# A mixture-of-experts layer on one core: the last expert's second product, combination and stores by halves of the columns

## Chip, cores, metric

One NeuronCore of a Trainium2 chip runs the whole layer in one launch. The metric is the device time of one execution in microseconds, as the median of several runs. The engines are TensorE (PE, its weight loads PEld), VectorE (DVE), ScalarE (ACT), GpSimd (POOL) and SyncE (SP), which issues the transfers that are spoken of here.

## What is computed

A layer over 512 latent tokens of 1024 channels with 256 context tokens: a DeltaNet mixer and latent attention, merged and added to the residual, and then sixteen experts of which each chooses 64 of the 512 tokens. The change touches the experts alone, and there the last of them:

```python
def expert_choice_moe(h, router_w, w_gate, w_up, w_down):
    cap = EC_CAPACITY * n_tok // N_EXPERTS                      # 64
    affinity = jax.nn.softmax((h @ router_w).astype(F32), axis=-1)
    gate, idx = lax.top_k(jnp.swapaxes(affinity, 1, 2), cap)
    xe = jax.vmap(lambda hb, ib: hb[ib])(h, idx)
    hid = jax.nn.silu(jnp.einsum('becd,edf->becf', xe, w_gate)) * jnp.einsum('becd,edf->becf', xe, w_up)
    ye = jnp.einsum('becf,efd->becd', hid, w_down) * gate[..., None].astype(h.dtype)
    return jax.vmap(lambda ib, yb: jnp.zeros((n_tok, d), yb.dtype).at[ib.reshape(-1)].add(yb.reshape(-1, d)))(idx, ye)

x = x_mid + mod_x[5] * expert_choice_moe(h2, ...)
```

w_gate and w_up are 1024 x 1408 per expert, w_down is 1408 x 1024, all in 32-bit floats.

## The kernel before

The experts run one after the other, from expert 0 to 15 (the loop at L1730). SP loads each expert's weights through a ring of nine buffers of 3072 columns (`piece`, L1709): four pieces of w_gate, four of w_up (each two blocks of 128 rows), then w_down in pieces of three blocks and a rest. A piece's transfer waits until TensorE is done with what lay in its buffer nine pieces before.

For an expert, TensorE multiplies its 64 tokens (XE, 128 rows by 64 columns of weights for the array) with w_gate into the PSUM tiles pg and with w_up into pu: the *first product*. The array is used as two halves of 64 columns each: the lower half of a row of weights goes to PSUM rows 0 to 63 (L1750), the upper to rows 64 to 127 (L1751), the two in turn, as pieces of 320 and 448 columns. ScalarE and VectorE make silu(pg) * pu of it in hd (L1769, L1771), TensorE turns it into hT by transposes (tile pt, L1774 to L1778, copied by L1775 to L1780).

The *second product* (tile pd, L1791) is hT times w_down: eleven blocks of 128 rows, and for each block columns 0 to 511 go to rows 0 to 63 of pd and columns 512 to 1023 to rows 64 to 127, again in turn:

```python
for dh in range(2):
    nc.tensor.matmul(pd[64 * dh:64 * dh + 64], l_, w[:, j, dh * 512:(dh + 1) * 512],
                     start=(i == 0), stop=(i == 10))
```

VectorE scales pd by gate and channel factor (L1795), ScalarE rounds the result to the type of the fast matmul (L1796), and VectorE takes the difference (L1797), so that the tile yo holds a high and a low part. The *combination* (tile pc, L1807) spreads the 64 rows over the 512 tokens: for each of four token tiles t and each half dh of the columns, one matmul of the high and one of the low part with the one-hot matrix oT; the rows of half dh lie on partitions 64 dh to 64 dh + 63. VectorE adds pc to the residual xm[t] (L1811). Experts are combined in pairs; 14 and 15 each by themselves. pc has two buffers of the tag "c"; expert 15's combination also borrows those of pg and pu. After expert 15 each half tile is stored as soon as it is added (L1813). A half tile is written (t, dh) below.

Apart from those lines of the program that are recorded through `TE`, `SE`, `VE` (a wrapper, `_Pinned`, that keeps an engine's instructions in program order among themselves and against what stands before them), the order on each engine is set by the tile scheduler, which lets matmuls of the next expert's first product stand between those of a combination.

Of the kernel before, what the change touches and what calls it, by code (L numbers as in the profile page):

```python
# [11 lines left out]
F32 = mybir.dt.float32  # L12
# [8 lines left out]
P = 128  # L21
# [11 lines left out]
NE = 16  # L33
# [141 lines left out]
def hybrid_block(ctx: ExitStack, tc: tile.TileContext, I, out, dbg=None):  # L175
# [1551 lines left out]
    GSTEP.update({(e, "w_gate", k0): 1 for e in (1, 2, 4, 5, 8, 9) for k0 in (0, 4)})  # L1727
    CH = ((0, 320), (320, 448))
    ys_ = []
    for e in range(NE):  # L1730
        pg = [pe([P, 448], "g", f"pg{e}{c}") for c in range(2)]
        pu = [pe([P, 448], "u", f"pu{e}{c}") for c in range(2)]
        for nm, dst in (("w_gate", pg), ("w_up", pu)):
            ko = (2, 4, 6, 0) if e == 0 and nm == "w_gate" else (0, 2, 4, 6)
            for k0 in ko:
                for _ in range(GSTEP.get((e, nm, k0), 0)):
                    next(ga, None)
                src = I[nm][0, e, k0 * P:(k0 + 2) * P, :].rearrange("(k p) f -> p k f", p=P)
                if e == 0 and nm == "w_gate" and k0 in (0, 6):
                    w = [halves[k0], halves[k0 + 1]]  # L1740
                else:
                    w = piece(FF, f"{nm}{e}_{k0}")
                    with tc.issue_after(issued["half" if PRM["p2"] else "woraw16"]):
                        nc.sync.dma_start(w, src)
                    w = [w[:, kk] for kk in range(2)]
                for kk in range(2):
                    k = k0 + kk
                    x_ = XE[:, e // GE % 2, k, (e % GE) * CAP:(e % GE + 1) * CAP]
                    for c, (o, n) in enumerate(CH):
                        nc.tensor.matmul(dst[c][0:64, :n], x_, w[kk][:, o:o + n], start=(k == ko[0]), stop=(k == ko[3] + 1))  # L1750
                        nc.tensor.matmul(dst[c][64:128, :320], x_, w[kk][:, FA + c * 320:FA + c * 320 + 320],  # L1751
                                         start=(k == ko[0]), stop=(k == ko[3] + 1))
        og = ex.tile([P, 4, 2, CAP], F32, tag="og", name=f"og{e}")
        for t in range(4):
            nc.vector.tensor_scalar(og[:, t], K("iota").unsqueeze(1).to_broadcast([P, 2, CAP]), slot[:, t, e:e + 1],
                                    aff[:, t, e:e + 1], op0=OP.is_equal, op1=OP.mult)
        p_ = pe([P, 4, P], "t", f"pog{e}", 1)
        for t in range(4):
            nc.tensor.transpose(p_[:, t], og[:, t].rearrange("p d s -> p (d s)"), ident)
        yo = ex.tile([P, 3, 512], F32R, tag="yo", name=f"yo{e}", bufs=2)  # L1760
        oT = yo[:, 2].rearrange("p (t s) -> p t s", t=4)
        nc.vector.tensor_scalar(oT, p_, 0.0, None, op0=OP.is_gt)
        gs = ex.tile([P, 1], F32, tag="gs", name=f"gs{e}", bufs=2)
        nc.vector.reduce_sum(gs, p_.rearrange("p t s -> p (t s)"), axis=AX.X)
        hh = ex.tile([P, 2, FA], F32, tag="hd", name=f"hd{e}", bufs=2)
        hd, hT = hh[:, 0], hh[:, 1].rearrange("p (b m) -> p b m", m=P)
        regs = ((0, slice(0, 128), 0, 320, 0), (1, slice(0, 128), 0, 320, 320), (1, slice(0, 64), 320, 448, 640))
        for c, pr, a, b, o in regs:
            nc.scalar.activation(hd[pr, o:o + b - a], pg[c][pr, a:b], AF.Silu)  # L1769
        for c, pr, a, b, o in regs:  # L1770
            nc.vector.tensor_mul(hd[pr, o:o + b - a], hd[pr, o:o + b - a], pu[c][pr, a:b])  # L1771
        p_ = pe([P, 4, P], "t", f"pt{e}0", 1)
        for b in range(4):
            nc.tensor.transpose(p_[:, b], hd[:, b * P:(b + 1) * P], ident)  # L1774
        nc.vector.tensor_copy(hT[:, 0:4], p_)  # L1775
        p_ = pe([P, 4, P], "t", f"pt{e}1", 1)
        nc.tensor.transpose(p_[:, 0], hd[:, 4 * P:5 * P], ident)
        nc.tensor.transpose(p_[:, 1, 0:64], hd[0:64, 5 * P:6 * P], ident[0:64, 0:64])  # L1778
        nc.vector.tensor_copy(hT[:, 4], p_[:, 0])
        nc.vector.tensor_copy(hT[:, 5, 0:64], p_[:, 1, 0:64])  # L1780
        pd = pe([P, 512], "d", f"pd{e}", 1)
        order = [(0, b) for b in range(6)] + [(1, b) for b in range(5)]
        for i0, n in ((0, 3), (3, 3), (6, 3), (9, 2)) if e < NE - 1 else ((0, 3), (3, 3), (6, 3), (9, 1), (10, 1)):
            w = piece(D, f"wd{e}_{i0}")
            nc.sync.dma_start(w[:, :n], I["w_down"][0, e, i0 * P:(i0 + n) * P, :].rearrange("(k p) d -> p k d", p=P))
            for j in range(n):
                i = i0 + j
                half, b = order[i]
                l_ = hT[:, b, half * 64:half * 64 + 64]
# [3 lines that stand above are left out]
        y = yo  # L1793
        yf = hd[:, 0:512]
        nc.vector.scalar_tensor_tensor(yf, pd, gs, m5, op0=OP.mult, op1=OP.mult)  # L1795
        nc.scalar.activation(y[:, 0], yf, AF.Copy)  # L1796
        nc.vector.tensor_sub(y[:, 1], yf, y[:, 0].bitcast(F32))  # L1797
        ys_.append((y, oT))
        if e % 2 or e == 14:
            for t in range(4):  # L1800
                tag = "cguc"[t] if e == 15 else "c"
                pcs = [pe([P, 512], tag, f"pc{e}{t}{dh}") for dh in range(2)]
                for i, (y_, o_) in enumerate(ys_):
                    for l in range(2):
                        for dh in range(2):
                            ps_ = slice(64 * dh, 64 * dh + 64)
                            nc.tensor.matmul(pcs[dh], o_[ps_, t, :], y_[ps_, l, :],  # L1807
                                             start=(i + l == 0), stop=(i + l == len(ys_)))
                for dh in range(2):
                    sl = slice(dh * 512, (dh + 1) * 512)  # L1810
                    nc.vector.tensor_add(xm[t][:, sl], xm[t][:, sl], pcs[dh])  # L1811
                    if e == NE - 1:
                        nc.sync.dma_start(out[0, t * P:(t + 1) * P, sl], xm[t][:, sl])  # L1813
            ys_ = []


# [22 lines left out]
```

## Time and profile before

| | |
|---|---|
| median of 3 runs | 1757.81 us (1753.52 to 1760.07) |
| the profiled execution | 1760.15 us |
| its span, first to last instruction | 1758.2 us |
| PE busy | 1590.3 us (90%) |
| DVE, ACT, POOL busy | 871.2, 593.5, 249.8 us |
| HBM read | 366.51 MB |

The page gives busy time by engine, the span in 40 slices, the chain of work that ended last, and the costliest groups of instructions. A timeline row has the start in us from the span's start, the time that it covers in us, engine, line, operation, output and inputs, rows and columns of the weights, rows and columns of the streamed operand, the count of records merged into it, and in brackets how long its engine stood idle before it and for what. A matmul in plain 32-bit floats leaves two records. The granted clock (PEclk) is a share of 2.4 GHz: 1.00 is 2.4 GHz, 0.50 is 1.2 GHz.

### The profile page before, as it was taken

To read this page: it belongs to the slowest core of one execution; us is meant where nothing else is said; L and a number is where in the kernel's file an instruction comes from. 1 tells how busy PE (TensorE), PEld (TensorE's weight loads), DVE (VectorE), ACT (ScalarE), POOL (GpSimd) and SP (SyncE) were. 2 spreads that over 40 slices of the span, in tenths; PEclk is the share of its full clock that TensorE was granted. 3 is DMA by queue.
4 is the path that set the end of the run, shared out by engine and by line. 5 is a ranking of instruction groups with operands and counts; after the bars stand their busy time and mean duration, and the time that the engine had idled before them with its cause. 6 is when DMAs were issued, how large, how long until landed. Compare 5 with 4: busy or idle time off the path is not lost.

```text
span 1758.2 us, 25301 instructions
## 1 busy us (share of the span) xinstructions
PE 1590.3 (90%) x9990; PEld 1096.7 (62%) x9990; DVE 871.2 (50%) x1926; ACT 593.5 (34%) x1362; POOL 249.8 (14%) x330
## 2 busy tenths in 40 slices
PE   5999998997999997989899996999999999989897
PEld 4687897785788786767687775544444454434343
DVE  3588758856978663757773446131212122212122
ACT  4676437425554344655674323100000010000000
POOL 2322022112121023222202522000000000000000
PEclk8999999998999998999899998999999999999999
DMA  9121302342222442030127945899999999999997
GB/s 324 49 61 37 110 24 61 96 145 84 61 67 79 136 138 66 26 109 21 46 72 234 287 171 208 328 413 412 413 412 413 413 413 413 413 413 413 414 413 288
DMA packets 168408, 382.30 MB, mean 217 GB/s; under 512 B 10373, under 2 KB 91491, under 8 KB 168291
## 3 DMA queue, kind: packets, MB, share of 16 engines
q1 hardware_dynamic: 163328, 372.98, 56.9%
q10 hardware_dynamic: 4963, 7.72, 1.4%
q8 instruction: 78, 1.28, 0.3%
q14 instruction: 39, 0.32, 0.1%
HBM read 366.51 MB, written 14.16 MB: 217 GB/s over the span
## 4 chain that ended last, share of the span: by engine, by line
PE 50%; DVE 9%; DMA 8%; ACT 4%; issue 3%; POOL 2%; SPq 0%; DVEq 0%; ACTq 0%; POOLq 0%
PE pd L1791 8%; PE pg L1750 6%; PE pu L1750 5%; DMA wd<-in_w_down_dram 4%; PE pg L1751 3%; PE pu L1751 3%; PE pc L1807 2%; DMA w_up<-in_w_up_dram 1%; PE pxe L1693 1%; PE pxe L1694 1%; PE px L140 1%; PE px L141 1%; PE px L142 1%; PE pPT L1337 1%; DMA raw_ukv<-in_w_ukv_dram 1%
## 5 line engine op out<-in xcount | busy, mean ns | idle before, releaser
L1750 PE MATMUL pg<-w_gate,XE 128*64 128x320 f32 x496 | 176.3, 505 | 1.1 <-DMA w_gate<-in_w_gate_dram 1.1
L1750 PE MATMUL pu<-w_up,XE 128*64 128x320 f32 x480 | 160.1, 487 | 5.2 <-DMA w_up<-in_w_up_dram 5.2
L1771 DVE TENSOR_TENSOR hd<-hd,pu 128x320 f32<-128x320 f32 (+1 forms) x48 | 18.6, 416 | 287.1 <-PE pu L1751 269.9
L1751 PE MATMUL pg<-w_gate,XE 128*64 128x320 f32 x496 | 154.0, 449 | 0.0
L1751 PE MATMUL pu<-w_up,XE 128*64 128x320 f32 x480 | 153.1, 444 | 0.0
L1791 PE MATMUL pd<-wd,hd 128*64 128x512 f32 x668 | 150.8, 597 | 1.6 <-DMA wd<-in_w_down_dram 1.6
L1796 ACT ACTIVATE yo<-hd 128x512 fp32r<-128x512 f32 x16 | 10.1, 629 | 344.2 <-DVE hd L1795 344.2
L1750 PEld LDWEIGHTS pu<-w_up,XE 128*64 128x64 f32 x480 | 64.6, 137 | 75.3 <-issue 37.3
L1791 PEld LDWEIGHTS pd<-wd,hd 128*64 128x64 f32 x668 | 44.8, 136 | 85.3 <-issue 76.0
L1750 PEld LDWEIGHTS pg<-w_gate,XE 128*64 128x64 f32 x496 | 65.8, 140 | 46.1 <-issue 23.2
L1769 ACT ACTIVATE hd<-pg 128x320 f32<-128x320 f32 (+1 forms) x48 | 16.5, 377 | 171.3 <-PE pg L1751 171.3
L1751 PEld LDWEIGHTS pg<-w_gate,XE 128*64 128x64 f32 x496 | 59.6, 137 | 23.2 <-issue 9.2
L1807 PE MATMUL pc<-yo 64*128 64x512 f32 x256 | 46.7, 450 | 26.1 <-ACT yo L1796 22.7
L1807 PEld LDWEIGHTS pc<-yo 64*128 64x128 f32 x256 | 23.1, 193 | 66.6 <-ACT yo L1796 35.9
L1811 DVE TENSOR_TENSOR xm<-xm,pc 128x512 f32<-128x512 f32 x72 | 45.9, 683 | 32.1 <-PE pc L1807 32.1
L1795 DVE SCALAR_TENSOR_TENSOR hd<-pd,gs,m 128x512 f32<-128x512 f32 x16 | 12.0, 751 | 96.3 <-PE pd L1791 96.3
L1697 ACT ACTIVATE XE<-pxe,mod,gs 128x256 f32<-128x256 f32 x32 | 16.3, 561 | 110.9 <-PE pxe L1694 98.2
L140 PE MATMUL pl_gt<-ht,wh_gt 128*128 128x512 f32 x128 | 52.6, 411 | 0.0
L142 PE MATMUL pl_gt<-ht,wl_gt 128*128 128x512 f32 x128 | 52.0, 406 | 0.0
L1751 PEld LDWEIGHTS pu<-w_up,XE 128*64 128x64 f32 x480 | 50.0, 135 | 3.1
L141 PE MATMUL pl_gt<-ht,wh_gt 128*128 128x512 f32 x128 | 51.4, 401 | 0.0
L1186 DVE TENSOR_TENSOR PT<-pPT,PT 128x512 fp32r<-128x512 f32 x48 | 33.0, 687 | 25.0 <-ACT PT L1185 24.8
(630 smaller groups left out, 4211.0 us busy)
## 6 DMA issues: line engine op xcount, KB each, us to landing
w_gate<-in_w_gate_dram SPq DMA_DIRECT2D x60, 1408.0 KB, 16.7
w_up<-in_w_up_dram SPq DMA_DIRECT2D x60, 1408.0 KB, 21.5
wd<-in_w_down_dram SPq DMA_DIRECT2D x45, 1536.0 KB
aw<-in_ada_w_dram SPq DMA_DIRECT2D x32, 512.0 KB, 4.7
wd<-in_w_down_dram SPq DMA_DIRECT2D x15, 1024.0 KB, 16.8
aq<-in_ada_w_dram SPq DMA_DIRECT2D x8, 1024.0 KB, 8.5
raw_gt<-in_w_in_dram SPq DMA_DIRECT2D x16, 512.0 KB, 3.8
ring_w<-in_w_up_dram SPq DMA_DIRECT2D x3, 1408.0 KB, 12.2
```

What stands on the lines that cost most here:

```text
L140: nc.tensor.matmul(out, wh, xh, start=first, stop=False)
L141: nc.tensor.matmul(out, wh, xl, start=False, stop=False)
L142: nc.tensor.matmul(out, wl, xh, start=False, stop=last)
L1186: nc.vector.tensor_sub(lo, src, hi.bitcast(F32))
L1337: nc.tensor.transpose(p_[:, t * P:(t + 1) * P], Pm[:, t, kt_ * P:(kt_ + 1) * P], ident)
L1693: nc.tensor.matmul(px[:, j], X2[:, t, 0, ks], oh, start=(t == 0), stop=False)
L1750: nc.tensor.matmul(dst[c][0:64, :n], x_, w[kk][:, o:o + n], start=(k == ko[0]), stop=(k == ko[3] + 1))
L1751: nc.tensor.matmul(dst[c][64:128, :320], x_, w[kk][:, FA + c * 320:FA + c * 320 + 320], start=(k == ko[0]), stop=(k == ko[3] + 1))
L1771: nc.vector.tensor_mul(hd[pr, o:o + b - a], hd[pr, o:o + b - a], pu[c][pr, a:b])
L1791: nc.tensor.matmul(pd[64 * dh:64 * dh + 64], l_, w[:, j, dh * 512:(dh + 1) * 512], start=(i == 0), stop=(i == 10))
L1807: nc.tensor.matmul(pcs[dh], o_[ps_, t, :], y_[ps_, l, :], start=(i + l == 0), stop=(i + l == len(ys_)))
L1811: nc.vector.tensor_add(xm[t][:, sl], xm[t][:, sl], pcs[dh])
```

## The change

For expert 15 alone:

- All its TensorE work is recorded through `TE`, that is, in program order and behind everything that stands before it.
- w_down comes as five pieces of half the columns: six and five blocks of columns 0 to 511, then six, three and two blocks of columns 512 to 1023 (rows of 2 KB, not 4 KB). The second product does the eleven blocks of the first half into one PSUM tile (tag "d"), then those of the second half into another (tag "t").
- The first half's values are made, combined and, for tiles 0 and 1, stored while the second half is still being multiplied: its combination for (0,0) and (1,0) stands between the sixth and the seventh block of the second half. The second half's values are made in two pieces of 256 columns.
- Three half tiles, (2,0), (3,0) and (1,1), get their residual before, by a matmul of xm with the identity into the PSUM tile of the combination (`carry`): two ahead of the third and fourth piece of w_up, one between the two groups of transposes. They are then copied out by ScalarE in place of an addition on VectorE.

```diff
+        if m == 512:
+            return w.rearrange("p (k f) -> p k f", k=6)
...
+    def carry(t, dh, tag):
+
+        bank[t, dh] = pe([P, 512], tag, f"pc{LAST}{t}{dh}")
+        TE.matmul(bank[t, dh], ident, xm[t][:, dh * 512:(dh + 1) * 512], start=True, stop=False)
+
+    def last_down(e, hT, hd, yo, oT, gs):
...
+        pds = [pe([P, 512], tag, f"pd{e}{dh}", 1) for dh, tag in enumerate("dt")]
+        held = {(2, 0), (3, 0), (1, 1)}
+        rest = {(0, 0): "g", (1, 0): "u", (0, 1): "u", (2, 1): "d", (3, 1): "t"}
+        rows = [slice(0, 64), slice(64, 128)]
+
+        def down(dh, i0, n):
+            w = piece(512, f"wd{e}_{i0}_{dh}")
+            nc.sync.dma_start(w[:, :n], I["w_down"][0, e, i0 * P:(i0 + n) * P, dh * 512:(dh + 1) * 512].rearrange("(k p) d -> p k d", p=P))
+            for j in range(n):
+                half, b = divmod(i0 + j, 6)
+                TE.matmul(pds[dh][rows[dh]], hT[:, b, half * 64:half * 64 + 64], w[:, j],
+                          start=(i0 + j == 0), stop=(i0 + j == 10))
+
+        def values(dh, cols):
+            r, yf = rows[dh], hd[:, 0:512]
+            for a, b in cols:
+                VE.scalar_tensor_tensor(yf[r, a:b], pds[dh][r, a:b], gs[r], m5[r, a:b], op0=OP.mult, op1=OP.mult)
+                SE.activation(yo[r, 0, a:b], yf[r, a:b], AF.Copy)
+            for a, b in cols:
+                VE.tensor_sub(yo[r, 1, a:b], yf[r, a:b], yo[r, 0, a:b].bitcast(F32))
+
+        def add(t, dh, l, cols=((0, 512),)):
...
+            for a, b in cols:
+                TE.matmul(bank[t, dh][:, a:b], oT[rows[dh], t, :], yo[rows[dh], l, a:b],
+                          start=(t, dh) not in held and l == 0 and a == 0, stop=(l == 1 and b == 512))
+
+        def store(t, dh):
+            xo = xm[t][:, dh * 512:(dh + 1) * 512]
+            if (t, dh) in held:
+                SE.activation(xo, bank[t, dh], AF.Copy)
+            else:
+                VE.tensor_add(xo, xo, bank[t, dh])
+            nc.sync.dma_start(out[0, t * P:(t + 1) * P, dh * 512:(dh + 1) * 512], xo)
+
+        down(0, 0, 6)
+        down(0, 6, 5)
+        values(0, ((0, 512),))
+        down(1, 0, 6)
+        for t in range(2):
+            add(t, 0, 0)
+            add(t, 0, 1)
+            store(t, 0)
+        down(1, 6, 3)
+        down(1, 9, 2)
+        two = ((0, 256), (256, 512))
+        values(1, two)
+        for t in (2, 3):
+            add(t, 0, 0)
+            add(t, 0, 1)
+            store(t, 0)
+        add(0, 1, 0, two)
+        add(1, 1, 0)
+        for t in range(4):
+            if t >= 2:
+                add(t, 1, 0)
+            add(t, 1, 1)
+            store(t, 1)
+
     for e in range(NE):
+        pe_ = TE if e == LAST else nc.tensor
...
+                if (e, nm) == (LAST, "w_up") and k0 >= 4:
+                    carry(k0 // 2, 0, "c")
...
+        if e == LAST:
+            carry(1, 1, "g")
...
+        if e == LAST:
+            last_down(e, hT, hd, yo, oT, gs)
+            break
...
-                tag = "cguc"[t] if e == 15 else "c"
-                pcs = [pe([P, 512], tag, f"pc{e}{t}{dh}") for dh in range(2)]
+                pcs = [pe([P, 512], "c", f"pc{e}{t}{dh}") for dh in range(2)]
...
-                    if e == NE - 1:
-                        nc.sync.dma_start(out[0, t * P:(t + 1) * P, sl], xm[t][:, sl])
```

How TensorE's instructions stand, at two places. First the start of expert 15's first product, TensorE, before (pc_13198 to pc_13207 are halves of expert 14's combination, pg_13230 and pg_13231 the last expert's first product):

```order
L1807 MATMUL pc_13198<-yo_13142 128x512 [waits DVE_49]
L1807 MATMUL pc_13199<-yo_13142 128x512
L1750 MATMUL pg_13230<-w_gate_0_13234,XE 64x320 [waits DMAHW1_49]
L1751 MATMUL pg_13230<-w_gate_0_13234,XE 64x320
L1750 MATMUL pg_13231<-w_gate_0_13234,XE 64x448
L1807 MATMUL pc_13206<-yo_13142 128x512 [waits DVE_49]
L1807 MATMUL pc_13207<-yo_13142 128x512 [waits DVE_49]
L1807 MATMUL pc_13206<-yo_13142 128x512
L1807 MATMUL pc_13207<-yo_13142 128x512
L1751 MATMUL pg_13231<-w_gate_0_13234,XE 64x320
```

The same place in the change:

```order
L1888 MATMUL pc_13199<-yo_13142 128x512
L1888 MATMUL pc_13206<-yo_13142 128x512 [waits DVE_49]
L1888 MATMUL pc_13206<-yo_13142 128x512
L1888 MATMUL pc_13207<-yo_13142 128x512 [waits DVE_49]
L1888 MATMUL pc_13207<-yo_13142 128x512
L1888 MATMUL pc_13214<-yo_13142 128x512 [waits DVE_49]
...
L1888 MATMUL pc_13223<-yo_13142 128x512 [waits DVE_49]
L1888 MATMUL pc_13223<-yo_13142 128x512
L153 MATMUL pg_13230<-w_gate_0_13234,XE 64x320 [waits DMAHW1_49]
L153 MATMUL pg_13230<-w_gate_0_13234,XE 64x320
```

All of expert 14's combination now stands ahead of the first pg, its two halves of a tile one after the other and no longer in turn (L153 is the line of the recording wrapper).

Second, TensorE from the third piece of w_up to the end, in the change (pc_13296, pc_13308 and pc_13345 are the carried half tiles, pd_13352 and pd_13353 the two halves of the second product). The second product before, w_down's first piece: 

```order
L1791 MATMUL pd_13346<-wd_0_13347,hd_13328 64x512 [waits DMAHW1_49]
L1791 MATMUL pd_13346<-wd_0_13347,hd_13328 64x512 x5
L1791 MATMUL pd_13346<-wd_3_13355,hd_13328 64x512 [waits DMAHW2_49]
```

and the change:

```order
L153 MATMUL pc_13308<-xm_9412,cst_81 128x512 [waits DVE_49]
L153 MATMUL pu_13232<-w_up_6_13306,XE 64x320 [waits DMAHW0_49]
...
L153 MATMUL pd_13352<-wd_0_0_13354,hd_13332 64x512 [waits DMAHW1_49]
L153 MATMUL pd_13352<-wd_6_0_13362,hd_13332 64x512 [waits DMAHW2_49]
L153 MATMUL pd_13352<-wd_6_0_13362,hd_13332 64x512 x4
L153 MATMUL pd_13353<-wd_0_1_13372,hd_13332 64x512 [waits DMAHW3_49]
L153 MATMUL pd_13353<-wd_0_1_13372,hd_13332 64x512 x5
L153 MATMUL pc_13380<-yo_13328 128x512 [waits Activation_49]
L153 MATMUL pc_13385<-yo_13328 128x512 x2
L153 MATMUL pd_13353<-wd_6_1_13390,hd_13332 64x512 [waits DMAHW4_49]
L153 MATMUL pd_13353<-wd_9_1_13395,hd_13332 64x512 [waits DMAHW5_49]
```

The matmuls of one half (always the same 64 rows of PSUM) follow each other; before, six from a piece were three blocks of the two halves in turn. Four combination matmuls, of (0,0) and (1,0), stand inside the second half.

## Rows read from the trace of the kernel before

**Rows 1.** The page: GB/s in 40 slices of the span.

```profile
GB/s 324 49 61 37 110 24 61 96 145 84 61 67 79 136 138 66 26 109 21 46 72 234 287 171 208 328 413 412 413 412 413 413 413 413 413 413 413 414 413 288
```

**Rows 2.** Timeline of the last expert from its transposes to the stores.

```profile
1735.32 0.33 PE L1777 MATMUL pt<-cst,hd 128*128 128x128 f32 x1 [0.79 <-DVE hd L1775]
...
1735.78 5.37 PE L1791 MATMUL pd<-wd,hd 128*64 128x512 f32 x24
...
1742.11 4.51 PE L1791 MATMUL pd<-wd,hd 128*64 128x512 f32 x20 [0.96 <-DMA wd<-in_w_down_dram]
1746.67 0.75 DVE L1795 SCALAR_TENSOR_TENSOR hd<-pd,gs,m 128x512 f32<-128x512 f32 x1 [10.36 <-PE pd L1791]
1747.46 0.63 ACT L1796 ACTIVATE yo<-hd 128x512 fp32r<-128x512 f32 x1 [25.57 <-DVE hd L1795]
1748.12 0.69 DVE L1797 TENSOR_TENSOR yo<-hd,yo 128x512 fp32r<-128x512 f32 x1 [0.70 <-ACT yo L1796]
1748.14 3.33 PE L1807 MATMUL pc<-yo 64*128 64x512 f32 x16 [1.52 <-ACT yo L1796]
1749.40 4.87 DVE L1811 TENSOR_TENSOR xm<-xm,pc 128x512 f32<-128x512 f32 x8 [0.59 <-PE pc L1807]
1750.12 4.52 SPq L1813 DMA_DIRECT2D out_dram<-xm  x8
```

**Rows 3.** Windows: stretch, its length, PE, PEld, DVE, ACT, POOL busy, PEclk, DMA, GB/s.

```profile
1744.00:1750.00 6.00, 4.48 (x26) 1.57 (x22) 2.04 (x3) 0.63 (x1) 0.00 (x0) 1.00 0.00 0
1752.00:1754.00 2.00, 0.00 (x0) 0.00 (x0) 2.00 (x4) 0.00 (x0) 0.00 (x0) 1.00 1.04 383
```

**Rows 4.** Timeline: single records of the last expert's two products.

```profile
1743.02 0.60 PE L1791 MATMUL pd<-wd,hd 128*64 128x512 f32 x2
...
1732.52 0.54 PE L1750 MATMUL pu<-w_up,XE 128*64 128x448 f32 x1
1732.58 0.43 PE L1751 MATMUL pu<-w_up,XE 128*64 128x320 f32 x1
1732.80 0.49 DVE L1771 TENSOR_TENSOR hd<-hd,pu 128x320 f32<-128x320 f32 x1 [16.84 <-PE pu L1751]
1732.89 0.54 PE L1750 MATMUL pu<-w_up,XE 128*64 128x448 f32 x1
...
1733.56 0.68 DVE L1771 TENSOR_TENSOR hd<-hd,pu 128x320 f32<-128x320 f32 x2 [0.27 <-PE pu L1751]
```

**Rows 5.** Timeline from expert 14's combination to the last piece of w_up.

```profile
1706.75 1.28 DVE L1811 TENSOR_TENSOR xm<-xm,pc 128x512 f32<-128x512 f32 x2 [0.59 <-PE pc L1807]
...
1709.33 1.10 PE L1807 MATMUL pc<-yo 64*128 64x512 f32 x4
...
1710.47 1.29 DVE L1811 TENSOR_TENSOR xm<-xm,pc 128x512 f32<-128x512 f32 x2 [2.44 <-PE pc L1807]
...
1711.81 0.74 PE L1807 MATMUL pc<-yo 64*128 64x512 f32 x4
...
1712.57 1.29 DVE L1811 TENSOR_TENSOR xm<-xm,pc 128x512 f32<-128x512 f32 x2 [0.81 <-PE pc L1807]
...
1721.08 0.43 PE L1750 MATMUL pu<-w_up,XE 128*64 128x320 f32 x1
...
1727.15 0.48 PE L1750 MATMUL pu<-w_up,XE 128*64 128x320 f32 x1 [0.74 <-DMA w_up<-in_w_up_dram]
...
1730.64 0.48 PE L1750 MATMUL pu<-w_up,XE 128*64 128x320 f32 x1 [0.69 <-DMA w_up<-in_w_up_dram]
```

**Rows 6.** Windows around that combination, and two of the DeltaNet stage.

```profile
1703.40:1706.70 3.30, 1.55 (x10) 0.43 (x6) 1.44 (x2) 0.63 (x1) 0.00 (x0) 1.00 1.01 413
1706.80:1710.10 3.30, 3.30 (x10) 1.04 (x8) 1.24 (x2) 0.00 (x0) 0.00 (x0) 0.50 1.03 420
...
348.20:351.60 3.40, 3.40 (x100) 2.25 (x100) 0.44 (x2) 0.58 (x2) 0.00 (x0) 0.50 0.50 151
351.60:355.00 3.40, 3.40 (x66) 2.85 (x59) 3.21 (x10) 0.00 (x0) 0.00 (x0) 0.50 0.03 8
```

More of the change, by code (lines that the diff above doesn't have):

```diff
@@ L1729, in hybrid_block @@
     ys_ = []
+    LAST = NE - 1
+    bank = {}
+    def carry(t, dh, tag):
[21 more added lines that the diff above has]
+        def add(t, dh, l, cols=((0, 512),)):
+            if (t, dh) not in bank:
+                tag = rest[t, dh]
+                bank[t, dh] = pe([P, 512], tag, f"pc{e}{t}{dh}", 2 if tag in "gu" else 1)
+            for a, b in cols:
[31 more added lines that the diff above has]
+            store(t, 1)
@@ L1749, in hybrid_block @@
                     for c, (o, n) in enumerate(CH):
-                        nc.tensor.matmul(dst[c][0:64, :n], x_, w[kk][:, o:o + n], start=(k == ko[0]), stop=(k == ko[3] + 1))
-                        nc.tensor.matmul(dst[c][64:128, :320], x_, w[kk][:, FA + c * 320:FA + c * 320 + 320],
+                        pe_.matmul(dst[c][0:64, :n], x_, w[kk][:, o:o + n], start=(k == ko[0]), stop=(k == ko[3] + 1))
+                        pe_.matmul(dst[c][64:128, :320], x_, w[kk][:, FA + c * 320:FA + c * 320 + 320],
                                          start=(k == ko[0]), stop=(k == ko[3] + 1))
@@ L1773, in hybrid_block @@
         for b in range(4):
-            nc.tensor.transpose(p_[:, b], hd[:, b * P:(b + 1) * P], ident)
+            pe_.transpose(p_[:, b], hd[:, b * P:(b + 1) * P], ident)
         nc.vector.tensor_copy(hT[:, 0:4], p_)
+        if e == LAST:
+            carry(1, 1, "g")
         p_ = pe([P, 4, P], "t", f"pt{e}1", 1)
-        nc.tensor.transpose(p_[:, 0], hd[:, 4 * P:5 * P], ident)
-        nc.tensor.transpose(p_[:, 1, 0:64], hd[0:64, 5 * P:6 * P], ident[0:64, 0:64])
+        pe_.transpose(p_[:, 0], hd[:, 4 * P:5 * P], ident)
+        pe_.transpose(p_[:, 1, 0:64], hd[0:64, 5 * P:6 * P], ident[0:64, 0:64])
         nc.vector.tensor_copy(hT[:, 4], p_[:, 0])
         nc.vector.tensor_copy(hT[:, 5, 0:64], p_[:, 1, 0:64])
+        if e == LAST:
+            last_down(e, hT, hd, yo, oT, gs)
+            break
         pd = pe([P, 512], "d", f"pd{e}", 1)
         order = [(0, b) for b in range(6)] + [(1, b) for b in range(5)]
-        for i0, n in ((0, 3), (3, 3), (6, 3), (9, 2)) if e < NE - 1 else ((0, 3), (3, 3), (6, 3), (9, 1), (10, 1)):
+        for i0, n in ((0, 3), (3, 3), (6, 3), (9, 2)):
             w = piece(D, f"wd{e}_{i0}")
```

## The prediction

> **What bounds the kernel now.** I read first the page's line of bytes per second: from the 27th slice to the last but one it stands at 412 to 414 GB/s [rows 1]; the sixteen experts run at the speed at which their weights arrive. Only what lies behind the last weights, or makes TensorE late for them, can move the end. Next the timeline of the last expert [rows 2]: the second product (tile pd) starts at 1735.78, waits 0.96 us for weights and ends at 1746.62 (1742.11 + 4.51). Then come three small steps, eight additions to the residual and eight stores: from 1746.62 to the end of the span, 1758.2, are 11.58 us, and the DMA engines stand idle until the stores begin [rows 3]. Then I read single records, for what TensorE gets out of two halves of its columns side by side [rows 4], and last the combination of expert 14 and the granted clock around it [rows 5, 6].
>
> **C, the second product by halves: +8.9 us.** Before, the matmuls of the two halves (pd rows 0 to 63 and 64 to 127) alternate; the change does eleven of one half, then eleven of the other. Rows 4 show two pd records beginning together: two halves of the array run at once. A matmul of this type leaves two records; the 24 of rows 2 are six blocks times two halves times two and take 5.37 us, so each half has twelve in 5.2 us (0.17 of drain taken off): one every 0.43 us. Is that the price of a pair, or of each half alone? A 448-column record is followed by the next of its half after 0.37 us (1732.52, 1732.89), the same pace per column, while its neighbour streams 320 columns only and stands still in between [rows 4]. The last one, of 1732.89, has no neighbour left, and its reader on VectorE starts at 1733.56. At 0.37 us the stream ends at 1733.26, and 0.30 remains for drain and hand-off. At twice the pace it would end at 1733.08, and VectorE, free at 1733.29 (1732.80 + 0.49), would have begun some 0.2 us sooner. So a lone half does not speed up, and each of the 44 records costs 0.43. After: 44 x 0.43 = 18.9, less 0.4 where the halves meet and overlap, plus 0.2 of drain, plus four combination matmuls now in between (16 in 3.33 us [rows 2], some 0.2 each, 0.8) and 0.2 for the two changes of shape: 19.7 us. Before: 10.84, its 0.96 of waiting included. Bounds: 8.5 (shape changes free) to 9.5.
>
> The weights don't decide it: by 1744 they had all landed [rows 3], and the last piece is now read about 17 us into the product, near 1757. Cut to 2 KB rows, the 5.77 MB may move at the 383 GB/s of the stores, which have such rows [rows 3], and not at 413: 15.1 against 14.0 us, 1 us, hidden by those 13 us, and added to the end if they were gone. SP issues five transfers as before and is then idle until the first store; twice the rows may take it longer, under the same cover.
>
> **A, expert 14's combination in one block: +3.6 us.** The order shows it: the last expert's TensorE work is kept in program order, so expert 14's combination (twelve matmuls, of tiles 1 to 3, stood between first-product matmuls) is now done before the first product begins. Two buffers and VectorE pace it. Additions follow each other at 0.60 us (eight in 4.87 [rows 2]), so one lasts 0.68 (1.28 - 0.60 [rows 5]). One round is an addition, a hand-off of 0.05, and from matmul to addition 0.76 at 2.4 GHz (1711.81 to 1712.57) or 1.14 at 1.2 GHz (1709.33 to 1710.47) [rows 5]: 1.5 or 1.9 us. The second addition ends at 1708.03; two rounds, a hand-off and two matmuls more, and the first product starts at 1711.6, or 1712.7 at the low clock. It is 8 blocks x 2 records x (0.37 + 0.27) = 10.3 us at full clock (0.27 is 0.37 x 320/448) and ends in rows 5 at 1721.08, where pu begins. At full clock it would now end 0.8 us later.
>
> But the clock was 1.2 GHz here: after a stretch in which PE was busy 1.55 us of 3.3 it stood at 0.50 from 1706.8 to 1710.1, with pairs of the first product filling PE [rows 6]; by 1711.81 the records are quick again [rows 5]. The stretch now holds lone matmuls and waits in their place. From 348.2 to 351.6 PE was busy throughout, with a hundred records, all but a few of them 32 x 32 pieces, the clock at 0.50, and it was 0.50 still in the row behind [rows 6]: such work need not bring it back. So I expect the low clock until pairs have streamed for as long as that row, some 3.3 us, of which 1.7 are lost: 1712.7 + 10.3 + 1.7 = 1724.7, +3.6 us. Bounds: 0.8 (full clock throughout) and 5.3 (low for twice as long).
>
> **B, the three carries (residual through TensorE): 0.** Each is two records of 512 columns, 0.86 us. Two stand ahead of the waits for w_up, where PE idles 0.74 and 0.69 us, 0.17 of drain each not counted [rows 5]. With A the data is there first: the two waits (1.77) vanish, the carries (1.72) take their place; without A they are nearly covered. The third fills the 0.79 us in which PE waits for the copy of the transposes [rows 2]. Bounds 0 to 0.5.
>
> **D, behind the second product: -2.8 us.** Six of the eight output halves are still open then; the two stored before share VectorE and SP with nothing urgent. The values go by quarters, each step priced at the whole row less half its column time (0.75, 0.63, 0.69 [rows 2]): scaling 0.5, rounding 0.4, again 0.4, difference 0.45, with hand-offs 1.9 us. Another 0.5 to the first of three VectorE additions: the last ends 4.3 us behind the product, before 7.65 (1749.40 + 4.87). ScalarE's three copies, 0.63 each as its row of 512 columns, queue behind its roundings and end at 2.0, 2.65 and 3.3. So six stores follow from 2.05 on, faster than they can move: 262,144 bytes at 383 GB/s [rows 3] are 0.68 us. Before: first issue 3.50 us behind the product (1750.12), eight x 0.68, and a rest of 2.6 make 11.58. After: 2.05 + 6 x 0.68 + 2.6 = 8.8. Bounds: -3.8 (the end follows the last addition, 3.9 us as before, and some) to -1.8 (copies and values a third dearer).
>
> **Sum:** 3.6 + 0 + 8.9 - 2.8 = +9.7 us. The profiled execution took 1760.15 us (span 1758.2), 2.3 above the median of the runs: 1769.9 against it, **1767.5 us** against the median of 1757.81.
>
> **Rivals.**
> 1. *The clock stays up around the combination.* For: PE's pauses there are short, and how they lie against the clock's changes will differ from run to run. Against: it fell in this profile [rows 6], and A empties that stretch further. A is 0.8 and the sum +6.9: 1764.7 us. Chance 0.25.
> 2. *A lone half streams twice as fast,* the pairs having only shared one stream: 512 columns in 0.23, near the pace of the combination's matmuls [rows 2]. Then C is 44 x 0.23 = 10.1 plus 1.0 in between and 0.2, 11.3 against 10.84: +0.5. The sum is 3.6 + 0.5 - 2.8 = +1.3, with rival 1 as well -1.5: **not slower**, 1756 to 1759 us. It decides if records of one half follow each other in under 0.25 us. Against it: the reader's start at 1733.56 [rows 4]. Chance 0.07. The Trainium skill, "TensorE: Matmul & The Clock Gate", Back-to-back issue gap, gives 216 ns for an isolated 512-column matmul at full clock; by that figure, as an estimate, 44 records take 9.5 us and the sum comes out here. The trace has 0.43 for these records, and the measurement decides.
> 3. *The low clock covers the second product too:* only half the array works in it, and if the clock falls at the pauses around the transposes it may not come back. 18.9 us of streams would double. Against: pairs stream up to the transposes, and the third carry fills a pause. If it holds half of the product, +9.5 more: 1777 us. Chance 0.06.
>
> **How the numbers follow.** Forecast 0.62, rivals 0.25, 0.07, 0.06. A measurement of this kernel tells about 0.5%, 8.8 us, from no change; the forecast lies just above that line, rival 1 below it. Of the forecast's 0.62 some 0.43 lie above (A's bounds are wide), and with rival 3 (0.06) and 0.06 of rival 1, where C or D is dearer, slower has 0.55. Faster needs rivals 1 and 2 and a lucky run: 0.03. The rest, 0.42, is the same. The range goes from A at full clock with C and D at their good ends (0.8 + 8.5 - 3.8 = +5.5, 1763.3) to all at their bad ends (5.3 + 0.5 + 9.5 - 1.8 = +13.5, 1771.3), each about 1 us further for the spread of the runs (1753.5 to 1760.1): **1762 to 1772 us**. It leaves out rivals 2 and 3.
>
> **What would show it.** Right: pd records of one half 0.43 us apart, none starting together but where the halves meet; the second product about 19.7 us long; no wait for w_up or w_down in the last expert; the first product ending 3 to 5 us later with a clock of 0.50 over its start; 9 us from the product's end to the span's, not 11.6. Wrong: records 0.22 us apart (C falls); the first product ending within 1 us of before (A falls); a clock of 0.50 in the second product (rival 3); a wait for w_down (2 KB rows cost more than 13 us).

## The result, and the profile after

Median 1769.82 us of 6 runs (1765.35 to 1772.96) against 1758.8 of 6 of the kernel before: ratio 1.0062, 95% interval 1.0039 to 1.0086, slower by some 11 us (7 to 15 by that interval). The profiled execution took 1770.05 us, its span 1768.1; the prediction had 1769.9 for that execution and 1767.5 for the median.

The page's line of bytes per second, as [rows 1]: the weights still come at 413 GB/s, and of their stretch, from the 27th slice on, only the last slice has changed (192, before 288).

```profile
GB/s 322 48 60 37 111 22 60 96 146 82 72 55 89 145 122 61 54 91 13 56 71 276 263 138 232 365 414 413 413 413 413 413 413 413 413 414 413 413 413 192
```

The timeline of the kernel after, from expert 14's values to the last stores; it answers to [rows 2, 4, 5]. Columns as there. L153 is the recording wrapper; a count can be a few records short.

```profile
1703.45 0.75 DVE L1877 SCALAR_TENSOR_TENSOR hd<-pd,gs,m 128x512 f32<-128x512 f32 x1 [5.97 <-PE pd L1873]
...
1706.18 1.28 DVE L1892 TENSOR_TENSOR xm<-xm,pc 128x512 f32<-128x512 f32 x2 [0.59 <-PE pc L1888]
1706.92 1.81 PE L1888 MATMUL pc<-yo 64*128 64x512 f32 x4 [0.78 <-DVE xm L1892]
1708.18 1.28 DVE L1892 TENSOR_TENSOR xm<-xm,pc 128x512 f32<-128x512 f32 x2 [0.71 <-PE pc L1888]
...
1712.67 11.97 PE L153 MATMUL pg<-w_gate,XE 128*64 128x320 f32 x63
1724.15 0.70 PE L153 MATMUL pu<-w_up,XE 128*64 128x320 f32 x2
...
1724.84 5.32 PE L153 MATMUL pu<-w_up,XE 128*64 128x320 f32 x30
1730.10 1.12 PE L153 MATMUL pc<-xm,cst 128*128 128x512 f32 x2
1731.15 2.79 PE L153 MATMUL pu<-w_up,XE 128*64 128x320 f32 x16
1733.88 1.12 PE L153 MATMUL pc<-xm,cst 128*128 128x512 f32 x2
...
1737.66 0.44 PE L153 MATMUL pt<-cst,hd 128*128 128x128 f32 x2
1738.67 1.02 PE L153 MATMUL pc<-xm,cst 128*128 128x512 f32 x2
...
1740.08 13.14 PE L153 MATMUL pd<-wd,hd 128*64 128x512 f32 x34
1742.70 5.31 PE L153 MATMUL pd<-wd,hd 128*64 128x512 f32 x12
1747.42 2.37 PE L153 MATMUL pd<-wd,hd 128*64 128x512 f32 x9
...
1753.15 1.21 PE L153 MATMUL pc<-yo 64*128 64x512 f32 x4
1754.29 4.50 PE L153 MATMUL pd<-wd,hd 128*64 128x512 f32 x10
...
1760.20 1.09 ACT L153 ACTIVATE xm<-pc 128x512 f32<-128x512 f32 x2
1760.83 3.08 SPq L1778 DMA_DIRECT2D out_dram<-xm  x6
1761.22 1.98 DVE L153 TENSOR_TENSOR xm<-xm,pc 128x512 f32<-128x512 f32 x3 [0.59 <-PE pc L153]
```

The two rows of 1742.70 and 1747.42 are pieces of the product on a shorter stretch: twelve records in 5.31 us, so (5.31 - 0.59) / 11 = 0.43 from one to the next, where only one half is at work (0.59 is what one record covers by itself); and nine records in 2.37, where the halves meet: in a row they would have taken 8 x 0.43 + 0.59 = 4.03.

Windows of the kernel after, columns as [rows 6, 3]: the low clock over the combination and the start of the first product, the full clock in the second product, the stores and what is left behind them.

```profile
1703.00:1706.00 3.00, 1.26 (x6) 0.37 (x4) 1.44 (x2) 0.63 (x1) 0.00 (x0) 1.00 1.02 415
1706.20:1709.50 3.30, 2.39 (x5) 1.49 (x6) 2.55 (x4) 0.00 (x0) 0.00 (x0) 0.50 1.02 418
1713.00:1716.30 3.30, 3.30 (x13) 1.83 (x11) 0.47 (x1) 0.00 (x0) 0.00 (x0) 0.50 1.01 411
1716.50:1719.80 3.30, 3.30 (x25) 1.79 (x22) 0.00 (x0) 0.00 (x0) 0.00 (x0) 1.00 1.03 420
1744.00:1750.00 6.00, 6.00 (x19) 2.08 (x18) 0.23 (x1) 0.00 (x0) 0.00 (x0) 1.00 0.00 1
...
1765.50:1766.50 1.00, 0.00 (x0) 0.00 (x0) 0.00 (x0) 0.00 (x0) 0.00 (x0) 0.50 0.34 117
1766.50:1767.50 1.00, 0.00 (x0) 0.00 (x0) 0.00 (x0) 0.00 (x0) 0.00 (x0) 0.50 0.01 4
```

**One clock for all kernels.** Expert 14's scaling step (the first row of the timeline) falls between 1695.2 and 1706.4 us in the eleven profiles of this case: a spread of some eleven us arises ahead of it, where no version has an edit. So all profiles are read from that step. The table gives, from there, when the last expert's first and second product begin, how long the second lasts (first record to end of the last, waits for weights included), what the end needs behind it, and the sum, which is the end of the span.

| us from expert 14's scaling step | first product begins | second begins | second lasts | behind it | sum |
|---|---|---|---|---|---|
| before | 2.6 | 31.76 | 10.84 | 11.58 | 54.18 |
| after | 9.2 | 36.63 | 18.72 | 9.31 | 64.66 |
| e1, product in pairs | 9.2 | 37.11 | 9.66 | 11.28 | 58.06 |
| e2, first product free | 2.6 | 32.28 | 18.70 | 9.32 | 60.30 |
| e3, before with halves only | 2.6 | 31.84 | 17.44 | 11.58 | 60.86 |
| e4, combination filled | 9.65 | 35.25 | 18.72 | 9.32 | 63.29 |
| e5, before with runs of three | 2.6 | 32.32 | 11.77 | 11.57 | 55.66 |
| e6, no carries | 9.2 | 34.32 | 18.72 | 8.99 | 62.02 |
| e7, pairs and first product free | 2.6 | 32.32 | 10.55 | 11.28 | 54.16 |
| e8, pause ahead filled | 8.5 | 36.16 | 18.72 | 9.32 | 64.20 |
| e9, halves, free, no carries | 2.6 | 32.54 | 18.70 | 8.99 | 60.24 |

By the rows the prediction used (the record of 1721.08 before, that of 1724.84 after): A is 21.39 - 17.06 = +4.3, B +0.5, C 18.72 - 10.84 = +7.9, D 9.31 - 11.58 = -2.3, together +10.5. The scaling step came 0.6 earlier after than before (1703.45, 1704.02), which leaves the +9.9 between the spans. Each row of the table is one profile of its version; e5 and e9 below show the begin of the second product move by 0.6 and 0.8 us with the arrival of the weights, so differences of that size between rows with such waits tell nothing.

### The profile page after: what moved, and what is told of

Read it like the earlier page. It is cut to its first block, busy times and chain, and to the rows that moved or that the text cites. A ratio compares the mean times of both kernels' runs of the same rounds, so it can differ in the third digit from the quotient of the medians.

```text
span 1768.1 us, 25322 instructions
## 1 busy us (share of the span) xinstructions
PE 1602.7 (91%) x9997; PEld 1099.3 (62%) x9997; DVE 869.2 (49%) x1927; ACT 595.9 (34%) x1367; POOL 249.5 (14%) x330
## 3 DMA queue, kind: packets, MB, share of 16 engines
q8 instruction: 78, 1.28, 0.3%
## 4 chain that ended last, share of the span: by engine, by line
PE 50%; DVE 10%; DMA 6%; ACT 3%; issue 3%; POOL 2%; SPq 0%; DVEq 0%; ACTq 0%; POOLq 0%
PE pd L1873 8%; PE pu L1827 6%; PE pg L1827 6%; PE pg L1828 3%; PE pu L1828 3%; PE pc L1888 2%; DMA wd<-in_w_down_dram 1%; DMA w_up<-in_w_up_dram 1%; PE pxe L1693 1%; PE pd L153 1%; PE pxe L1694 1%; PE pPT L1337 1%; DMA raw_ukv<-in_w_ukv_dram 1%; PE px L140 1%; DVE tmp L830 1%
## 5 line engine op out<-in xcount | busy, mean ns | idle before, releaser
L1827 PE MATMUL pg<-w_gate,XE 128*64 128x320 f32 x464 | 164.7, 505 | 1.1 <-DMA w_gate<-in_w_gate_dram 1.1
L1827 PE MATMUL pu<-w_up,XE 128*64 128x320 f32 x448 | 148.7, 487 | 2.8 <-DMA w_up<-in_w_up_dram 2.8
L1828 PE MATMUL pg<-w_gate,XE 128*64 128x320 f32 x464 | 144.5, 449 | 0.0
L1828 PE MATMUL pu<-w_up,XE 128*64 128x320 f32 x448 | 143.4, 444 | 0.0
L1873 PE MATMUL pd<-wd,hd 128*64 128x512 f32 x624 | 140.9, 597 | 0.5 <-DMA wd<-in_w_down_dram 0.5
L1827 PEld LDWEIGHTS pu<-w_up,XE 128*64 128x64 f32 x448 | 60.5, 137 | 68.1 <-issue 37.1
L1827 PEld LDWEIGHTS pg<-w_gate,XE 128*64 128x64 f32 x464 | 61.6, 140 | 44.9 <-issue 22.3
L1846 ACT ACTIVATE hd<-pg 128x320 f32<-128x320 f32 (+1 forms) x48 | 16.5, 378 | 177.2 <-PE pg L1828 157.4
L1828 PEld LDWEIGHTS pg<-w_gate,XE 128*64 128x64 f32 x464 | 55.7, 138 | 20.8 <-issue 8.5
L1892 DVE TENSOR_TENSOR xm<-xm,pc 128x512 f32<-128x512 f32 x64 | 41.1, 683 | 31.1 <-PE pc L1888 31.1
L1828 PEld LDWEIGHTS pu<-w_up,XE 128*64 128x64 f32 x448 | 46.1, 135 | 2.4
```

The source lines that it names most:

```text
L1827: pe_.matmul(dst[c][0:64, :n], x_, w[kk][:, o:o + n], start=(k == ko[0]), stop=(k == ko[3] + 1))
L1828: pe_.matmul(dst[c][64:128, :320], x_, w[kk][:, FA + c * 320:FA + c * 320 + 320], start=(k == ko[0]), stop=(k == ko[3] + 1))
```

## The experiments

The theory is the prediction's: the halves cost C since a lone half streams no faster, pinning costs A, and D gives some of it back. The rivals are those of the prediction, and that the parts hang together otherwise than by a sum. Each ratio is to runs of the kernel before that were taken with that version's.

**e1: the second product in pairs again.** The change with one tile pd, w_down in pieces of three blocks, the values in one go; the pinned order and the carries stay.

```diff
-        down(0, 0, 6)
...
+            for j in range(n):
+                half, b = divmod(i0 + j, 6)
+                for dh in range(2):
+                    TE.matmul(pd[rows[dh]], hT[:, b, half * 64:half * 64 + 64], w[:, j, dh * 512:(dh + 1) * 512],
```

> The changed kernel with its second product in pairs of halves again (one pd tile, w_down in pieces of three blocks, values made once for both halves); program order on TensorE, the three carries and ScalarE's copies stay. Theory (a lone half streams at 0.43 us a record, so the halves one after the other cost their sum): the product falls from 18.7 us in the changed kernel to 9.6 to 10 us; behind it eight stores instead of six, 11 to 11.6 us instead of 9.3; together 6 to 7 us less than the changed kernel, some 1763 us, still 4 above before because the first product stays late. Rival (the halves cost nothing, the first product's delay and the clock are the whole loss): the product stays within 1 us of 18, or the time doesn't fall, 1769 to 1772 us.

1761.92 us (ratio 1.0022, 0.9994 to 1.0049). The timeline of e1 has the product in one row, with no wait in it:

```profile
1742.26 9.66 PE L153 MATMUL pd<-wd,hd 128*64 128x512 f32 x44
```

So the pinned order, the carries and ScalarE's copies make +3.9 in the table; the interval of the medians alone would not tell that from nothing. Of the 5.35 us by which the second product starts later, 1.2 come back at once: it does not stand 0.96 for weights any more [rows 2].

**e2: the last expert's first product free.** The change, with the first product and the transposes not recorded in program order.

```diff
-        pe_ = TE if e == LAST else nc.tensor
+        pe_ = nc.tensor
```

> The changed kernel, with the last expert's first product and its transposes no longer kept in program order; everything else stays. Theory (the block of expert 14's combination makes the first product late, by itself and through the clock): in the trace the first product ends 4 us sooner relative to expert 14's values, the granted clock is 0.50 for at most 3.4 us there instead of 10.2, and the time is 4 us below the changed kernel, some 1765.5 us. Rival (the clock falls there anyway and the block costs little): first product less than 1.5 us sooner, 1768 us or more.

1762.58 us (ratio 1.0022, 1.0002 to 1.0041). The first product begins 2.6 us behind the scaling step as before, the second 0.5 later than before, and what follows is as in the change: A is undone alone, 4.35 us. The granted clock was 0.50 for 3.4 us around that combination, as before, and not for 10.2 as in the change. The medians put the same step at 7 (4.4 and 11.0 above their runs of before), each with some 4 us of uncertainty either way.

**e3: the kernel before, and only its last second product by halves.**

```diff
+            for dh, i0, n in ((0, 0, 6), (0, 6, 5), (1, 0, 6), (1, 6, 3), (1, 9, 2)):
...
+                    TE.matmul(pd[64 * dh:64 * dh + 64], hT[:, b, half * 64:half * 64 + 64], w[:, j],
```

> The kernel before with one edit: the last expert's second product by halves of the columns (five pieces of half columns, eleven blocks of one half, then eleven of the other, into one pd tile); first product, values, combination and stores as before. Theory: the product takes 44 records of 0.43 us less 1.7 us where the halves meet, 17.4 us with its drain, for 10.8: 6.6 us more than before, some 1765 us, the 11.6 us behind it unchanged. Rival (a lone half costs less when its PSUM tile is the same): product under 13 us, at most 2 us above before.

1765.35 us (ratio 1.0043, 1.0027 to 1.006). The timeline of e3:

```profile
1730.01 0.48 PE L1752 MATMUL pu<-w_up,XE 128*64 128x320 f32 x1 [0.74 <-DMA w_up<-in_w_up_dram]
...
1735.16 17.44 PE L153 MATMUL pd<-wd,hd 128*64 128x512 f32 x44
```

All else stands as before (start 31.84, end 11.58 behind), and the product is 17.44 us long and not 10.84. C is shown by itself. The change's 18.72 is this and 1.28 for the four combination matmuls in its middle.

**e5: the kernel before, in runs.** In each piece of w_down first the blocks of one half, then those of the other: runs of three matmuls, six records, on one half.

```diff
-            for j in range(n):
+            for j, dh in ([(j, dh) for dh in range(2) for j in range(n)] if e == NE - 1 else [(j, dh) for j in range(n) for dh in range(2)]):
```

> The kernel before, with the last expert's second product in runs: within each piece of w_down (three blocks) first the blocks of one half, then those of the other; same transfers, same tiles. If only records that stand next to each other overlap, as the prediction had it (0.4 us at each of nine changes of half), the product takes 44 x 0.43 - 9 x 0.43 = 15 us and the time grows by 4. If TensorE starts records of the other half past up to three waiting ones, as the changed kernel's trace shows where its halves meet, the second half lags by two records, 0.86 us, and otherwise streams beside the first: product 11 to 12 us, at most 1.5 us more than before. If halves overlap only in strict turn: 18 us, 7 more.

1757.5 us (ratio 1.0004, 0.9989 to 1.0019). The timeline of e5, its six and its last five blocks, split where the kernel before waits for weights [rows 2]:

```profile
1734.88 6.28 PE L153 MATMUL pd<-wd,hd 128*64 128x512 f32 x24
...
1741.23 5.42 PE L153 MATMUL pd<-wd,hd 128*64 128x512 f32 x20
```

Before, these were 5.37 and 4.51: +0.91 each, two records at 0.43 and a little. The whole product takes 11.77 us, where overlap of neighbours alone would have made it 15. So TensorE lets a record of one half start while records of the other, ahead of it in program order, still wait. The first +0.91 went into the wait for weights, which shrank to almost nothing.

This profile shows one thing more. Up to the second product its edit changes nothing, and yet the clock stayed at 1.00 around expert 14's combination; the same window of the kernel before, from the scaling step, has 0.50 [rows 6]:

```profile
1705.30:1708.60 3.30, 3.30 (x18) 1.14 (x18) 2.49 (x4) 0.00 (x0) 0.00 (x0) 1.00 1.01 415
1726.26 0.48 PE L1750 MATMUL pu<-w_up,XE 128*64 128x320 f32 x1 [2.06 <-DMA w_up<-in_w_up_dram]
```

So the clock need not fall there. The first record of pu came 15.4 us behind the scaling step (1717.94), before 16.5 (1720.55), but the gain was waited away: the waits for w_up are 0.66, 2.06 and 0.68 us, before 0.74 and 0.69, and the second product begins 0.6 later. Where TensorE waits for weights anyway, the quicker clock earned nothing.

**e6: no carries.** The change without the three, so that all eight additions are VectorE's.

```diff
-        held = {(2, 0), (3, 0), (1, 1)}
+        held = set()
...
-                if (e, nm) == (LAST, "w_up") and k0 >= 4:
-                    carry(k0 // 2, 0, "c")
```

> The changed kernel without the three carries: all eight output halves are added on VectorE. Theory (in the changed kernel the data is there before the carries, which cost their 1.7 us on TensorE, and the stores set the end): second product 1.2 to 1.8 us sooner, the end behind it 9.3 to 9.8 us, time 1 to 1.5 us below the changed kernel. Rival (ScalarE's copies pay): end behind the product 11 us or more, time above the changed kernel.

1765.34 us (ratio 1.0042, 1.0025 to 1.0059). The timeline of e6:

```profile
1720.68 10.48 PE L153 MATMUL pu<-w_up,XE 128*64 128x320 f32 x62
1731.10 0.44 PE L153 MATMUL pt<-cst,hd 128*128 128x128 f32 x2
...
1733.52 13.15 PE L153 MATMUL pd<-wd,hd 128*64 128x512 f32 x34
...
1754.10 3.68 DVE L153 TENSOR_TENSOR xm<-xm,pc 128x512 f32<-128x512 f32 x6
1754.82 3.32 SPq L1778 DMA_DIRECT2D out_dram<-xm  x6
```

From the w_up record (1720.68, the one that answers to 1724.84) to the transposes are 10.42 us (1720.68 to 1731.10) and no wait; in the change 12.82 (1724.84 to 1737.66). Two carries cost 2.4, 1.2 each, not 0.86. The third is free: from the transposes to the second product are 2.42 us in the change, in e6 and before. And the end is no later without them: 8.99 us against 9.31. So beside the pinned order the carries cost some 2.6 us and earned nothing; 1 to 1.5 were expected.

**e7: both undone, the carries kept** (e1 and e2 together).

> Both undone: the changed kernel with the product in pairs and the first product free; the carries and ScalarE's copies stay. Theory: what is left of the change is worth nothing or little: carries covered by the waits for w_up to 0.5 us, stores paced by their transfers, so that the end behind the product is 11 to 11.6 us: 1757 to 1760 us, as before. Rival (copies on ScalarE shorten the end): 9.5 us behind the product and 2 us below before.

1758.53 us (ratio 1.001, 0.999 to 1.0029), in the table 54.16 against 54.18. The product waits for weights again, as before:

```profile
1727.47 5.37 PE L153 MATMUL pd<-wd,hd 128*64 128x512 f32 x24
1733.51 4.51 PE L153 MATMUL pd<-wd,hd 128*64 128x512 f32 x20 [0.67 <-DMA wd<-in_w_down_dram]
```

Without the halves and the pinned order nothing of the loss is left. Where TensorE waits for weights, the carries are nearly covered: the second product starts 0.56 later, its wait is 0.3 shorter, and 0.3 less stands behind it, where the copies are on ScalarE.

**e4: the combination filled with idle matmuls.** The change, with matmuls into a tile that nobody reads before and between the matmuls of expert 14's combination, to hold the clock up.

```diff
+            for n in (256, 256, 256):
+                fill(n)
...
+                        if l == 1 and 0 < t < 3 or (l, dh) == (1, 0) and t == 3:
+                            fill(128)
```

> The changed kernel with idle matmuls added: the identity times a stretch of gathered tokens, into a PSUM tile that nothing reads, in the pauses before and inside expert 14's combination (three of 256 columns while TensorE waits for the values, then one or two short ones between the combination's matmuls). The order of the real work is that of the changed kernel. Theory (most of the late first product is the low clock): the granted clock stays 1.00 there, the first product ends 2.5 to 3.5 us sooner relative to expert 14's values than in the changed kernel, and the time is some 3 us below it, 1766 to 1767 us. Rival (the block and its two buffers make the delay): the clock stays up and the first product still ends within 1 us of the changed kernel's; the time is the same or 1 us more.

1767.81 us (ratio 1.0062, 1.0042 to 1.0082). Windows of e4, over the combination and over the first product:

```profile
1702.10:1711.80 9.70, 9.68 (x40) 5.64 (x38) 6.17 (x9) 0.63 (x1) 0.00 (x0) 1.00 1.02 416
1711.90:1721.40 9.50, 9.50 (x63) 5.33 (x63) 0.69 (x1) 0.00 (x0) 0.00 (x0) 1.00 1.02 413
```

and two rows of its timeline:

```profile
1711.84 10.16 PE L153 MATMUL pg<-w_gate,XE 128*64 128x320 f32 x63
1721.51 0.70 PE L153 MATMUL pu<-w_up,XE 128*64 128x320 f32 x2
```

The clock stayed at 1.00, and from the first product's start to the first w_up record the way is 9.67 us, not 11.48 (1712.67 to 1724.15): the low clock costs 1.8 us there. But PE was busy for 9.68 of the 9.70 us, so the fillers themselves held up the block (first product at 9.65, not 9.2). All in all -1.4, between the two expectations (2.5 to 3.5, and under 1). What the block costs at full clock, this run does not tell.

**e8: only the pause ahead of the combination filled.** The three idle matmuls of 256 columns, none inside the block.

```diff
+            for n in (256, 256, 256):
+                TE.matmul(fl[:, 0:n], ident, XE[:, 1, 0, 0:n], start=True, stop=True)
```

> The change, with three idle matmuls of 256 columns (a tile nobody reads) only in TensorE's 1.5 us pause for expert 14's values; the block of the combination itself is as in the change. If the block is dear because of the low clock alone, the granted clock stays at 1.00 through it, the block's rounds fall from 2.00 to about 1.5 us, the first product's start comes 7.6 to 8.2 us behind the scaling step (9.22 in the change), its 11.5 us fall to 9.7, and the first w_up record comes about 17.5 us behind the scaling step (20.70 in the change, 16.53 before): 3 us less of span, partly eaten by waits for w_up that come back. If the clock falls at the waits between the block's halves whatever stands before, all of it is as in the change within 0.3 us.

1768.1 us (ratio 1.0054, 1.0031 to 1.0076). Windows of e8:

```profile
1701.40:1705.40 4.00, 2.82 (x10) 1.19 (x10) 3.18 (x5) 0.00 (x0) 0.00 (x0) 1.00 1.03 421
1705.80:1712.40 6.60, 6.60 (x21) 3.42 (x21) 2.57 (x4) 0.00 (x0) 0.00 (x0) 0.50 1.02 416
```

and VectorE in its timeline, the additions of the combination:

```profile
1702.60 1.28 DVE L1896 TENSOR_TENSOR xm<-xm,pc 128x512 f32<-128x512 f32 x2 [0.59 <-PE pc L1892]
1704.10 1.29 DVE L1896 TENSOR_TENSOR xm<-xm,pc 128x512 f32<-128x512 f32 x2 [0.22 <-PE pc L1892]
1705.62 0.69 DVE L1896 TENSOR_TENSOR xm<-xm,pc 128x512 f32<-128x512 f32 x1 [0.22 <-PE pc L1892]
...
1707.61 0.69 DVE L1896 TENSOR_TENSOR xm<-xm,pc 128x512 f32<-128x512 f32 x1 [0.40 <-PE pc L1892]
```

Neither expectation held whole. The clock outlasted the first rounds (1702.60 to 1704.10 to 1705.62, 1.50 and 1.52 us) and fell inside the block; the next round took 1.99. The block gained 0.7 and the sum 0.5. So the block's own lone matmuls and waits are followed by the low clock even with a busy pause ahead.

**e9: halves, first product free, no carries** (e2 and e6 together).

> The change without its two losers beside the halves: the first product is not pinned and there are no carries. If the parts add up, from expert 14's scaling step: first product as before (second product about 31.8 us behind it), second product 18.7 us, end 9.0 us behind that: 59.5 against 54.2 before, so 5 us slower than before in the median (1762 where before is 1757), 5 faster than the change. If the parts hang together otherwise, the sum from the scaling step differs from 59.5 by over 1 us.

1765.13 us (ratio 1.0027, 1.0002 to 1.0053), in the table 60.24. The waits for w_up are back, the first longer than before's 0.74 [rows 5]:

```profile
1730.27 0.48 PE L1825 MATMUL pu<-w_up,XE 128*64 128x320 f32 x1 [1.50 <-DMA w_up<-in_w_up_dram]
1733.80 0.48 PE L1825 MATMUL pu<-w_up,XE 128*64 128x320 f32 x1 [0.74 <-DMA w_up<-in_w_up_dram]
```

These 0.76 us are about what it lies above the 59.5 expected: where TensorE waits for weights, it is their arrival that counts, not the way from the scaling step (so for e5 too). The parts add up to within the 1 us set for it. Of the nine, e5 and e7 come level with the kernel before, and none points to a version that beats it by what a measurement shows.

## Why the prediction was right

The mechanism held: the halves one after the other and the pinned order lose more than the shorter end gains. The sum, +9.7, stands against +10.5 from the scaling step and +11.0 between the medians. That it came so near is in part luck: C was set 1.0 too high, A, B and D 0.7, 0.5 and 0.5 too low, and these errors offset each other. That the profiled execution met its forecast within 0.2 us is chance: ahead of the change it was 0.6 us quicker than the profile of before.

**C, the halves: the mechanism held, the size was 1 us too large** (+8.9, measured +7.9). Records of a lone half stand 0.43 apart, and rival 2 (under 0.25) is out. The figure of 216 ns for an isolated 512-column matmul that the Trainium skill has ("TensorE: Matmul & The Clock Gate", Back-to-back issue gap) is not what these records do. The combination's matmuls, of the other type, come near it (16 in 3.33 us [rows 2]). The term that failed is "less 0.4 where the halves meet and overlap". There the first four records of the second half ran beside the last four of the first: the row of nine records in 2.37 us. Four times 0.43 is 1.7, not 0.4. The other way round, the four matmuls in between cost 1.28 (e3) where 0.8 and 0.2 were set. The trace of before could have told of the first. On its timeline the last expert's w_gate ends so:

```profile
1720.55 0.43 PE L1751 MATMUL pu<-w_up,XE 128*64 128x320 f32 x1
1720.71 0.54 PE L1750 MATMUL pg<-w_gate,XE 128*64 128x448 f32 x1
```

The pu record of the upper half (L1751) stands in the program behind two records of pu's lower half, the first of which is that of 1721.08 [rows 5], and behind the pg record of 1720.71. It starts ahead of all three. The prediction read rows 4 for the pace of a half and did not ask in which order the halves start.

**A, the pinned order: +4.3, set at +3.6, within its bounds of 0.8 to 5.3.** Expected were the first product at 8.7 us behind the scaling step (1712.7 less 1704.02) and 12.0 from there to the w_up record; it came at 9.2 and took 12.2. The rounds last 2.00 us (1706.18 to 1708.18), not 1.9. The low clock lasted through the combination and into the first product, as expected; e4 measures what that costs the product as 1.8 us (1.7 was set). Rival 1, a clock that stays up, did not come true in the change's profile, and e8 shows it fall even with the pause filled. It fell in all three profiles with the pinned order and nothing filled (the change, e1, e6), but with the order of before it stayed up in one (e5) of six: where it falls does differ from run to run, as that rival said.

**B, the carries: set at 0, within 0 to 0.5; the net is +0.5, at that bound: a price was too low.** The prediction has the two waits for w_up vanish through A (1.77) and the carries (1.72) take their place. The waits did vanish through A: e6 has neither carries nor waits, and from the w_up record to the second product it takes 12.84 us where before has 14.70, so 1.86 less. But the two carries cost 1.2 each and not 0.86, with the changes of shape around them: 2.4. That is the +0.5. The net hides what the carries are worth: the 1.86 are gained without them.

**D, behind the product: -2.3, set at -2.8.** The first of the six stores is issued 2.03 us behind the product (1760.83 less 1758.80; 2.05 was set), and by 1766 nearly all bytes were moved. What failed is the rest, "2.6" as before: 9.31 - 2.03 - 6 x 0.68 leaves 3.2, with a last few bytes moving at 4 GB/s beyond 1766.5. The last section has what stands beside that; without those 0.8 us of trickle, as an estimate, the rest is 2.4 and D -3.1.

**Rival 3** is out: the clock was 1.00 in the window of the second product (1744 to 1750), and 0.43 us from record to record is the pace of the full clock. No wait for w_down came, so the 2 KB rows stayed under their cover.

## What to carry to other kernels

Where two halves of the array work side by side, doing one half first costs nearly the whole time of the other: the split bought 2.3 us behind the product for 7.9 in it, and it could not have bought more than the 11.6 that stood there. If a change takes a wait away, that wait covers nothing any more: price in full what was to be done in it (here the carries). Where versions differ by a fraction of a per cent, read their profiles from a common event shortly ahead of the change; the medians of this kernel could not have told the parts apart.

## Not expected of the hardware

- A record for one half of the columns starts while up to three records of the other half, ahead of it in program order, still wait (1720.55 before), and where the halves meet four of them ran side by side. Runs of six records on one half, in turn, therefore cost only 0.91 us in each of the two rows of e5.
- Each of two carries, of two 512-column records, took 1.2 us of TensorE's time, between matmuls of the first product, which have another shape; two records of 0.43 are 0.86.
- With the halves and the copies on ScalarE together (the change, e2, e4, e8) the end came 9.31 or 9.32 us behind the product; without the carries (e6, e9) it came at 8.99, although their first store is issued later (2.58 against 2.03). Two views of the DMA queues follow. The first has the change's bytes in 40 slices of 1754 to 1769, with a trickle at their end (16, 16), and what an instruction queue, q14, moved there (packets, MB, share). The second has the bytes of e6 in 40 slices of 1747 to 1762, without the trickle:

```profile
GB/s 0 0 0 5 371 366 399 257 0 0 0 0 0 0 0 0 0 0 0 0 208 371 393 382 377 393 377 361 388 377 404 153 16 16 0 0 0 0 0 0
q14 instruction: 1, 0.01, 0.1%
...
GB/s 0 0 0 0 0 295 377 404 322 0 0 0 0 0 0 0 0 0 0 0 0 0 0 350 377 366 404 366 377 399 361 404 377 382 33 0 0 0 0 0
```

The trickle goes with that one packet, of 8 KB: in the change it moves between 1765.3 and 1765.8, towards the end of the last stores, and seven packets of the stores are left behind, until about 1766.7, where all else is done by 1765.9. In e2, e4 and e8 such a packet stands among the last six stores as well; in the seven profiles without the trickle none moves between the first of the last stores and the end. That the packet causes the trickle, by holding up a DMA engine that it shares with the stores, is likely but not shown, and why it falls there only with halves and copies together stays open.
